# Loading two rows of an expert's w1 per partition with one DMA, in a hybrid RG-LRU, sparse-attention and MoE layer

## The chip, the cores and the metric

The kernel runs on one core of a Trainium2 chip. The metric is the device time of one execution in microseconds (us), and the median over several runs is what kernels are compared by. The engines are called as the profile calls them: PE (TensorE; PEld is its weight loads), DVE (VectorE), ACT (ScalarE), POOL (GpSimd) and SP (SyncE, which here only issues DMAs). Sixteen DMA engines move data between the memory of the chip (HBM) and the core's SBUF.

## The reference

One layer works on 512 tokens of 1024 features, in f32. After a modulated RMSNorm come two parallel branches (an RG-LRU recurrence and an attention over the best 128 keys of each query), whose joined output is added to x. Then follows a mixture of 32 experts, of which each token uses 4. This is the part that the change touches:

```python
def moe_ffn(h, w_router, b_router, w1, b1, w2, b2):
    logits = (h @ w_router + b_router).astype(jnp.float32)
    top_val, top_e = lax.top_k(logits, TOPK_EXPERTS)          # 4 of 32
    gates = jax.nn.softmax(top_val, axis=-1).astype(h.dtype)
    ...
    def expert_block(args):
        tok, gate, e = args
        u = h_pad[tok] @ w1[e] + b1[e]                        # (1024) -> 2048
        u_glu = jnp.minimum(u[:, ::2], SWIGLU_LIMIT)
        u_lin = jnp.clip(u[:, 1::2], -SWIGLU_LIMIT, SWIGLU_LIMIT)
        act = u_glu * jax.nn.sigmoid(SWIGLU_ALPHA * u_glu) * (u_lin + 1)
        return (act @ w2[e] + b2[e]) * gate[:, None]          # (1024) -> 1024
```

Each expert has 8 MB of w1 and 4 MB of w2, so the 32 experts read 384 MB of weights, each byte once.

## The kernel before

The first 450 us or so do the norm, the input projection, the two branches, the output projection and the router. The rest of the time goes to the experts.

**The experts in order.** The experts are ranked by how many tokens chose them (the first two by number, so that their weights can be loaded before the router is done), and each gets 1 to 4 blocks of 32 token rows, by a fixed list. The list `NBS` of blocks in the order of work is 3, 3, 4, 2, 3, 2, 3, 4, 2, 3, 2, 3, and so on, and ends with 2, 1, 2, 1. There are 86 blocks in all. A loop at the end of the program takes tokens that found no room; it ran zero times in the profiled execution.

**One expert.** The loop from L974 interleaves neighbours. For expert j it gathers token rows two experts ahead (L859, POOL), loads w1 of j and multiplies (`up`, L888), applies the gated activation (`glu`, L893 to L897, DVE and ACT), turns the tokens of the next expert (`turn_x`, L867) and makes its bias (L874), loads w2 of expert j - 1 and multiplies (`down`, L915 and L921), scales and adds the result to the output by an accumulating indirect DMA (`add_out`, L930 and L932), and turns its own activations (`turn_act`, L905). Weights are the moving operand: `up` goes through 8 rows k of w1, each 128 x 2048, and for each row and block issues four matmuls of 32 columns by 512. The trace holds two records for each such f32 matmul, so a row of w1 with 4 blocks is 32 records, and with 1 block 8.

**The weight slots.** Weights lie in a ring of nine SBUF slots of 16 KB per partition:

```python
slots_at = (164, 148, R[0], R[1], R[3], R[2], R[5], R[4], R[6])
...
t = [mem(kb + 8 * j, blocks, n) for j in range(2)]
for j in range(2):
    nc.sync.dma_start(t[j], src(j))
```

Each slot holds two tiles of 8 KB per partition, and each tile is the target of one DMA of 1 MB: one row k of w1 (128 partitions x 8 KB) or one quarter of w2 (also 8 KB per partition). In HBM, partition p's eight rows of w1 lie one behind the other, 64 KB in a piece (`w1_of`, L950), and the DMA of one row takes 8 KB out of it. An expert takes six slots, four for w1 and two for w2.

**What sets the order.** All weight DMAs stand in one queue, SP's, in the order that the framework's scheduler gives them. Such a DMA is issued when three things hold: the DMA before it on SP has been issued; PE is through with what lay in that tile (the wait on PE); and the DMA that last used the same completion semaphore has landed. There are eight of these semaphores (DMAHW0 to DMAHW7), taken in turn, so at most eight of SP's DMAs are under way. PE waits for each weight DMA at the first matmul that reads its tile. The order of the instructions on every engine is also the scheduler's.

Of the kernel before, what the change touches and what calls it, by code (L numbers as in the profile page):

```python
# [18 lines left out]
S, D, H, HD, E, FF = 512, 1024, 8, 64, 32, 1024  # L19
# [18 lines left out]
def layer(ctx, tc, x, c, w_ada, b_ada, norm1_g, w_in, conv_w, conv_b, w_rg_a, b_rg_a, w_rg_x, b_rg_x,  # L38
          lru_lambda, q_norm_g, k_norm_g, kidx_norm_g, rg_out_g, attn_out_g, w_out, norm2_g,
          w_router, b_router, w1, b1, w2, b2, out, dbg=None):  # L40
    nc = tc.nc
    V, A, T, G = nc.vector, nc.scalar, nc.tensor, nc.gpsimd
# [15 lines left out]
    bk = [psp.tile([128, 512], F32, name=f"bank{i}") for i in range(8)]  # L58
# [6 lines left out]
    def mem(kb, *shape, dt=F32):  # L65

        n = 1
        for d in shape:
            n *= d
        key = (kb, n, dt)  # L70
        if key not in views:
            assert kb * 1024 % 32 == 0 and kb * 1024 + n * (2 if dt == BF else 4) <= nc.sbuf_usable_end - base
            views[key] = nc.alloc_sbuf_tensor_at(f"mem{len(views)}", [128, n], dt, offset=base + int(kb * 1024)).ap()
        v = views[key]
        if len(shape) > 1:
            names = "abcd"[:len(shape)]
            v = v.rearrange(f"p ({' '.join(names)}) -> p {' '.join(names)}", **dict(zip(names, shape)))
        return v
# [133 lines left out]
    xT = [mem(112 + 2 * k, S) for k in range(4)] + [mem(131.375 + 2 * k, S) for k in range(4)]  # L212
# [16 lines left out]
    for v in range(2):  # L229
        for k, g in [(k, g) for k in range(KD) for g in (2 * v, 2 * v + 1)]:  # L230
            t = ada[2 * (g // 2) + k // 4][:, k % 4, 512 * (g % 2):512 * (g % 2) + 512]
# [472 lines left out]
    BT = 32  # L704
# [15 lines left out]
    nslot = [0]  # L720
    slots_at = (164, 148, R[0], R[1], R[3], R[2], R[5], R[4], R[6])
# [97 lines left out]
    def wslot(blocks, n, src):  # L819
        nslot[0] += 1  # L820
        kb = slots_at[(nslot[0] - 1) % len(slots_at)]
# [3 lines that stand above are left out]
        return t  # L825
# [49 lines left out]
        A.copy(biasb[j % 2], p)  # L875

    def load_up(src):
        return [t for q in range(4) for t in wslot(1, 2 * FF, lambda j: src[:, 2 * q + j:2 * q + j + 1, :])]

    def load_down(src):  # L880
        return [t for q in range(2) for t in wslot(2, D, lambda j: src[:, 2 * q + j])]
# [1 line left out]
    def up(j, w, nb):  # L883
        xT = xTs[j % 2]
        for k in range(KD):
            for b in range(nb):
                for n in range(4):
                    T.matmul(bk[b][32 * n:32 * n + 32, :], xT[:, k, BT * b:BT * b + BT], w[k][:, 0, n * 512:(n + 1) * 512],  # L888
                             start=(k == 0), stop=(k == KD - 1))

    def glu(j, nb):
# [62 lines left out]
    def expert(j):  # L954

        if j < 2:
            return slice(j, j + 1)
        if j not in whose:
            whose[j] = nc.values_load(ids[0:1, j:j + 1], engines=[mybir.EngineType.SP], min_val=0, max_val=E - 1)
        return bass.ds(whose[j], 1)  # L960
# [13 lines left out]
    for j in range(E + 1):  # L974
        nb = NBS[j] if j < E else 0
        if j + 2 < E:
            gather(j + 2, xg_of(j + 2), NBS[j + 2])
        if j < E:
            w = load_up(w1_of(expert(j)))
            up(j, w, nb)  # L980
            glu(j, nb)
        if j + 1 < E:
            turn_x(j + 1, xg_of(j + 1), NBS[j + 1])
            bias(j + 1, bias_col(j + 1))
        if j == 0:
            gated_bias()
        if j:
            down(load_down(w2_of(expert(j - 1))), NBS[j - 1])
            add_out(j - 1, NBS[j - 1])
        if j < E:  # L990
            turn_act(nb)
        if j % 4 == 0 and j + 4 < E:
            route(j + 4, 4)
# [20 lines left out]
    with tc.For_i(0, blocks, 1):  # L1014
# [39 lines left out]
        turn_x(0, 0, 4)  # L1054
        bias(0, selb1)
        up(0, load_up(w1_of(bass.ds(ev, 1))), 4)
        glu(0, 4)
        turn_act(4)
# [26 lines left out]
```

## Time and profile before

| what | value |
|---|---|
| median of 3 runs | 1475.12 us (1473.19 to 1480.09) |
| profiled execution | 1474.65 us, of which the span from first to last instruction is 1472.7 us |
| PE busy | 1372.4 us (93% of the span), 10907 matmul records |
| of these `up`, L888 | 622.9 us, 5504 records |
| of these `down`, L915 and L921 | 270.6 and 60.7 us, 2304 and 448 records |
| DVE, ACT, POOL busy | 34%, 18%, 15% of the span |
| loads of w1 and w2 | 384 DMAs of 1024 KB, issued by SP at L824 |
| hardware queue of SP (q1) | 75582 packets, 453.73 MB, 76.9% of the 16 engines' time |
| mean granted clock of PE | 0.958 |

The busy time of an engine is the union of its instructions, each record lasting until the modelled end of its matmul, so PE can be "busy" while a matmul shares the array with three others. The share of the DMA engines is the summed time of their packets over 16 engines, and can pass 1 a little, because a packet begins shortly before the one ahead of it is done. In the strips of the page a slice is 36.8 us, and a digit is tenths.

### The profile page before, as it was taken

The numbers are of one execution on the slowest core, as the hardware profiler recorded it, in microseconds if no ns is written. First come the engines' busy times: TensorE is split into PE (matmuls) and PEld (weight loads), VectorE is DVE, ScalarE is ACT, GpSimd is POOL, SyncE is SP. The second block draws the span as 40 slices with busy tenths as digits, with TensorE's granted clock in tenths as the row PEclk, the third lists the DMA queues.
The fourth block names the chain that finished last, engine by engine and source line by source line (L and its number), as shares of the span: only waits on it lengthen the run. The fifth ranks groups of instructions, "written<-read, shape, count | busy, mean of one in ns | idle before, by whom it ended". The sixth has DMA issues, their size and how long they took to land. (4 is left out here: it accounts for less than half of the span.)

```text
span 1472.7 us, 26489 instructions
## 1 busy us (share of the span) xinstructions
PE 1372.4 (93%) x10907; PEld 622.2 (42%) x10907; DVE 498.2 (34%) x1266; ACT 265.1 (18%) x538; POOL 228.1 (15%) x248
## 2 busy tenths in 40 slices
PE   5899999999779999999999999999999999999984
PEld 2755787777623343333433333333333333333220
DVE  2668986845624122212222122122132112212211
ACT  2544653532201010000010010001010010100100
POOL 3313621711100111011101011000101011110100
PEclk9999999958689999999999999999999999999996
DMA  9667213007578999999999999999999999999995
GB/s 361 213 212 261 93 58 115 22 29 292 208 281 353 379 384 409 372 403 408 404 398 403 417 403 399 401 405 398 413 389 404 405 411 407 399 389 390 413 404 199
DMA packets 87274, 482.40 MB, mean 328 GB/s; under 512 B 11974, under 2 KB 14214, under 8 KB 37902
## 3 DMA queue, kind: packets, MB, share of 16 engines
q1 hardware_dynamic: 75582, 453.73, 76.9%
q0 software_dynamic: 10560, 24.68, 6.9%
q10 hardware_dynamic: 1008, 2.25, 0.4%
q8 instruction: 88, 1.44, 0.4%
q14 instruction: 36, 0.29, 0.1%
HBM read 465.14 MB, written 15.48 MB: 326 GB/s over the span
## 5 line engine op out<-in xcount | busy, mean ns | idle before, releaser
L888 PE MATMUL bank<-mem,mem 128*32 128x512 f32 x5504 | 622.9, 595 | 2.8 <-DMA mem<-in_w_dram 2.8
L888 PEld LDWEIGHTS bank<-mem,mem 128*32 128x32 f32 x5504 | 174.7, 110 | 373.8 <-issue 359.1
L915 PE MATMUL bank<-mem,mem 128*32 128x512 f32 x2304 | 270.6, 597 | 0.0
L893 DVE TENSOR_TENSOR bank<-bank,mem 128x512 f32<-128x512 f32 x86 | 59.9, 697 | 450.4 <-PE bank L888 450.3
L932 POOL DMA_INDIRECT out_dram<-mem,idx_h x50 | 76.7, 1534 | 733.1 <-DVE mem L930 573.6
L915 PEld LDWEIGHTS bank<-mem,mem 128*32 128x32 f32 x2304 | 88.2, 110 | 144.5 <-issue 133.6
L895 ACT ACTIVATE mem<-bank 128x256 f32<-128x256 f32 x86 | 33.1, 385 | 559.1 <-DVE bank L893 559.1
L157 PE MATMUL bank<-mem,mem 128*128 128x512 f32 (+1 forms) x320 | 114.6, 359 | 4.1 <-DVE mem L537 3.1
L158 PE MATMUL bank<-mem,mem 128*128 128x512 f32 (+1 forms) x320 | 112.4, 351 | 0.0
L159 PE MATMUL bank<-mem,mem 128*128 128x512 f32 (+1 forms) x320 | 111.4, 348 | 0.0
L930 DVE SCALAR_TENSOR_TENSOR mem<-bank,gate_h,mem 128x512 f32<-128x512 f32 x36 | 27.0, 750 | 213.2 <-PE bank L915 204.5
L157 PEld LDWEIGHTS bank<-mem,mem 128*128 128x128 f32 x320 | 61.8, 194 | 17.6 <-issue 4.8
L158 PEld LDWEIGHTS bank<-mem,mem 128*128 128x128 f32 x320 | 61.9, 193 | 11.7 <-issue 5.0
L159 PEld LDWEIGHTS bank<-mem,mem 128*128 128x128 f32 x320 | 61.7, 193 | 11.5 <-issue 5.6
L859 POOL DMA_INDIRECT mem<-h_d,idx_all x32 | 30.5, 954 | 222.8 <-PE bank L867 151.3
L921 PE MATMUL bank<-mem,mem 128*32 128x512 f32 x448 | 60.7, 593 | 2.3 <-SPq L1014 1.3
L867 PEld LDWEIGHTS bank<-ident,mem 128*128 128x128 f32 (+2 forms) x256 | 33.2, 196 | 62.7 <-issue 28.5
L867 PE MATMUL bank<-ident,mem 128*128 128x128 f32 (+2 forms) x256 | 42.5, 294 | 17.9 <-DMA mem<-h_d,idx_all 9.3
L868 DVE COPY mem<-bank 128x512 f32<-128x512 f32 (+2 forms) x32 | 18.0, 563 | 115.1 <-PE bank L867 112.7
L906 ACT COPY mem<-bank 128x512 f32<-128x512 f32 (+1 forms) x32 | 18.3, 573 | 207.5 <-PE bank L915 108.9
L153 POOL TENSOR_TENSOR mem<-mem,mem 128x512 fp32r<-128x512 f32 x24 | 34.4, 1453 | 89.8 <-ACT mem L152 89.7
L905 PEld LDWEIGHTS bank<-ident,mem 128*128 128x128 f32 x172 | 24.3, 207 | 38.3 <-issue 22.9
(327 smaller groups left out, 1212.8 us busy)
## 6 DMA issues: line engine op xcount, KB each, us to landing
mem<-in_w_dram SPq DMA_DIRECT2D x384, 1024.0 KB
mem<-in_w_ada_dram SPq DMA_DIRECT2D x16, 1024.0 KB
mem<-in_w_in_dram SPq DMA_DIRECT2D x20, 512.0 KB
mem<-in_w_ada_dram SPq DMA_DIRECT2D x3, 2048.0 KB
mem<-in_x_dram SPq DMA_DIRECT2D x8, 512.0 KB
mem<-in_w_out_dram SPq DMA_DIRECT2D x8, 512.0 KB
mem<-in_w_ada_dram SPq DMA_DIRECT2D x4, 512.0 KB
mem<-in_w_in_dram SPq DMA_DIRECT2D x8, 256.0 KB
```

The lines of the kernel that those rows point to most:

```text
L153: (sub or V).tensor_sub(lo, src, hi)
L157: T.matmul(p, ah, bh, start=(k == 0), stop=False)
L158: T.matmul(p, al, bh, start=False, stop=False)
L159: T.matmul(p, ah, bl, start=False, stop=(k == n - 1))
L859: G.indirect_dma_start(out=xgs[to][a], out_offset=None, in_=h2_d, in_offset=bass.IndirectOffsetOnAxis(ap=idx_all[a, r:r + 1], axis=0))
L867: T.transpose(p[:, k, 0:n], xgs[frm][0:n, 4 * q + k::KD], ident[0:n, 0:n])
L888: T.matmul(bk[b][32 * n:32 * n + 32, :], xT[:, k, BT * b:BT * b + BT], w[k][:, 0, n * 512:(n + 1) * 512], start=(k == 0), stop=(k == KD - 1))
L893: V.tensor_add(bk[b], bk[b], biasb[j % 2])
L895: A.activation(act[:, b], u[:, :, 0], AF.Gelu_apprx_sigmoid)
L915: T.matmul(bk[6 + b // 2][o:o + 32, :], aT[:, b, c, BT * n:BT * n + BT], w[n][:, c, m * 512:(m + 1) * 512], start=(n + c == 0), stop=(n == ...
L921: T.matmul(bk[6 + nb // 2][o:o + 32, :], aT[:, nb - 1, c, BT * n:BT * n + BT], w[n][:, c, m * 512:(m + 1) * 512], start=(n == 0), stop=(n ...
L932: G.indirect_dma_start(out=out_half, out_offset=bass.IndirectOffsetOnAxis(ap=idx_h[a, h, j:j + 1], axis=0), in_=ys[h][a], in_offset=None, ...
```

## The change

`load_up` no longer goes through `wslot`. It takes a slot of the ring as before, but as one tile of 2 x 2048 per partition, and fills it with one DMA of rows 2q and 2q + 1 of w1. Since the two rows lie one behind the other in HBM and in the tile, the DMA moves one piece of 16 KB per partition. `up` takes the two halves of the tile as rows. The loads of w2 (`load_down`) keep their two tiles and two DMAs per slot. The ring, its nine slots and the order in which slots are taken are unchanged.

```diff
     def load_up(src):
-        return [t for q in range(4) for t in wslot(1, 2 * FF, lambda j: src[:, 2 * q + j:2 * q + j + 1, :])]
+
+        w = []
+        for q in range(4):
+            nslot[0] += 1
+            t = mem(slots_at[(nslot[0] - 1) % len(slots_at)], 2, 2 * FF)
+            nc.sync.dma_start(t, src[:, 2 * q:2 * q + 2, :])
+            w += [t[:, j] for j in range(2)]
+        return w
...
-                    T.matmul(bk[b][32 * n:32 * n + 32, :], xT[:, k, BT * b:BT * b + BT], w[k][:, 0, n * 512:(n + 1) * 512],
+                    T.matmul(bk[b][32 * n:32 * n + 32, :], xT[:, k, BT * b:BT * b + BT], w[k][:, n * 512:(n + 1) * 512],
                              start=(k == 0), stop=(k == KD - 1))
```

On SP, the loads of expert 3's w1 and expert 2's w2 stand like this before; the last number is the tile's size, the register rows between the DMAs are left out, and in the brackets DMAHW is a completion semaphore and PE the release of the tile:

```order
L959 TENSOR_LOAD ids
...
L824 DMA mem_78<-in_w_dram 128x2048 [waits DMAHW0_49,PE_49]
...
L824 DMA mem_79<-in_w_dram 128x2048 [waits DMAHW1_49,PE_49]
...
L824 DMA mem_3563<-in_w_dram 128x2048 [waits DMAHW2_49,PE_49]
...
L824 DMA mem_3564<-in_w_dram 128x2048 [waits DMAHW3_49,PE_49]
...
L824 DMA mem_3216<-in_w_dram 128x2048 [waits DMAHW4_49,PE_49]
...
L824 DMA mem_3217<-in_w_dram 128x2048 [waits DMAHW5_49,PE_49]
...
L824 DMA mem_3220<-in_w_dram 128x2048 [waits DMAHW6_49,PE_49]
...
L824 DMA mem_3221<-in_w_dram 128x2048 [waits DMAHW7_49,PE_49]
```

And the same place after the change, with the four loads of w2 that follow:

```order
L966 TENSOR_LOAD ids
...
L883 DMA mem_133<-in_w_dram 128x4096 [waits PE_49]
...
L883 DMA mem_103<-in_w_dram 128x4096 [waits DMAHW6_49,DMAHW5_49,PE_49]
...
L883 DMA mem_3216<-in_w_dram 128x4096 [waits PE_49]
...
L883 DMA mem_3218<-in_w_dram 128x4096 [waits DMAHW7_49,PE_49]
...
L824 DMA mem_3966<-in_w_dram 128x2048 [waits DMAHW0_49,PE_49]
...
L824 DMA mem_3967<-in_w_dram 128x2048 [waits DMAHW1_49]
...
L824 DMA mem_3970<-in_w_dram 128x2048 [waits DMAHW2_49,PE_49]
...
L824 DMA mem_3971<-in_w_dram 128x2048 [waits DMAHW3_49]
```

Eight loads with a release each became four, each with one release for both rows; and where a pair of w2 tiles follows a w1 tile in its slot, only the first of the pair waits for PE, since the whole tile is given back at once.

The other place is the end of the program on PE. These are the last matmuls of the last expert, which has one block (`up` in bank_65), and of the two `down` steps behind it (bank_71), before the change:

```order
L888 MATMUL bank_65<-mem_78,mem_2672 32x512 x4
L888 MATMUL bank_65<-mem_79,mem_2672 32x512 x4
L905 MATMUL bank_69<-ident,mem_2934 128x128
L915 MATMUL bank_71<-mem_3563,mem_2931 32x512 x8
L905 MATMUL bank_69<-ident,mem_2934 128x128
L915 MATMUL bank_71<-mem_3564,mem_2931 32x512 x8
...
L921 MATMUL bank_71<-mem_3220,mem_2931 32x512 x4
L921 MATMUL bank_71<-mem_3221,mem_2931 32x512 x4
L921 MATMUL bank_71<-mem_3224,mem_2931 32x512 x4
L921 MATMUL bank_71<-mem_3225,mem_2931 32x512 x4
```

And after it:

```order
L895 MATMUL bank_65<-mem_134,mem_2672 32x512 x8
L895 MATMUL bank_65<-mem_133,mem_2672 32x512 x8
L922 MATMUL bank_71<-mem_3548,mem_2931 32x512 x8
L912 MATMUL bank_69<-ident,mem_2934 128x128 x2
L922 MATMUL bank_71<-mem_3549,mem_2931 32x512 x8
...
L928 MATMUL bank_71<-mem_9397,mem_2931 32x512 x4
L928 MATMUL bank_71<-mem_9398,mem_2931 32x512 x4
L928 MATMUL bank_71<-mem_3966,mem_2931 32x512 x4
L928 MATMUL bank_71<-mem_3967,mem_2931 32x512 x4
```

The last two rows of w1 now come in one tile, and the scheduler has put the first quarter of the `down` step of the expert before between `up` and the transposes of the activations (L905, now L912), where the transposes came first.

## Rows read from the trace of the kernel before

**Rows 1.** The page: DMA busy digits, rates in 40 slices, SP's hardware queue.
```profile
DMA  9667213007578999999999999999999999999995
GB/s 361 213 212 261 93 58 115 22 29 292 208 281 353 379 384 409 372 403 408 404 398 403 417 403 399 401 405 398 413 389 404 405 411 407 399 389 390 413 404 199
...
q1 hardware_dynamic: 75582, 453.73, 76.9%
```

**Rows 2.** Engine busy time by stretch; last three columns: PE clock, DMA share, GB/s.
```profile
core 0: us, PE busy (x) PEld busy (x) DVE busy (x) ACT busy (x) POOL busy (x), PEclk, DMA share, GB/s
...
480.00:505.00 25.00, 25.00 (x233) 8.82 (x229) 2.42 (x4) 1.17 (x2) 3.09 (x2) 1.00 1.02 398
505.00:530.00 25.00, 25.00 (x232) 10.16 (x228) 8.44 (x17) 3.56 (x8) 2.54 (x2) 1.00 0.97 349
...
700.00:900.00 200.00, 197.14 (x1764) 69.41 (x1760) 42.62 (x115) 17.98 (x38) 21.26 (x16) 1.00 1.02 405
...
1325.00:1350.00 25.00, 25.00 (x236) 7.68 (x232) 5.43 (x12) 1.54 (x4) 0.00 (x0) 1.00 0.99 391
...
1400.00:1436.00 36.00, 31.38 (x285) 9.65 (x281) 5.28 (x10) 2.31 (x5) 2.98 (x2) 0.99 1.02 404
...
1450.00:1455.00 5.00, 3.12 (x28) 0.66 (x24) 0.75 (x1) 0.37 (x1) 1.56 (x1) 1.00 0.67 199
```

**Rows 3.** What PE waited for, 520 to 1472 us: total, times, longest (two rows).
```profile
PE bank L888 <- DMA mem<-in_w_dram: 2.8, 2, 2.1
...
PE bank L921 <- SPq L1014: 1.3, 1, 1.3
```

**Rows 4.** PE in order of time, the end: start, length, what, [idle before <-releaser].
```profile
1426.61 5.33 PE L888 MATMUL bank<-mem,mem 128*32 128x512 f32 x48
1432.70 1.07 PE L888 MATMUL bank<-mem,mem 128*32 128x512 f32 x8 [0.76 <-DMA mem<-in_w_dram]
1435.85 1.93 PE L888 MATMUL bank<-mem,mem 128*32 128x512 f32 x8 [2.08 <-DMA mem<-in_w_dram]
...
1440.48 3.64 PE L915 MATMUL bank<-mem,mem 128*32 128x512 f32 x16
...
1451.14 2.94 PE L921 MATMUL bank<-mem,mem 128*32 128x512 f32 x24 [0.96 <-ACT mem L906]
...
1455.42 1.07 PE L921 MATMUL bank<-mem,mem 128*32 128x512 f32 x8 [1.34 <-SPq L1014]
```

**Rows 5.** DMA packets and mean rate, 37 to 43 us (w_in, 2 KB pieces).
```profile
DMA packets 1268, 2.44 MB, mean 407 GB/s; under 512 B 77, under 2 KB 77, under 8 KB 1268
```

**Rows 6.** The same, 16 to 26 us (w_ada, 4 KB pieces).
```profile
DMA packets 1067, 4.21 MB, mean 421 GB/s; under 512 B 40, under 2 KB 40, under 8 KB 1066
```

**Rows 7.** The same, 826 to 849 us (expert weights alone, 8 KB pieces).
```profile
DMA packets 1345, 9.79 MB, mean 426 GB/s; under 512 B 152, under 2 KB 152, under 8 KB 152
```

**Rows 8.** What SP waited for, 480 to 530 us (all its rows).
```profile
SPq L824 <- PE bank L888: 27.1, 10, 3.9
SPq L824 <- PE bank L921: 15.6, 7, 3.5
```

**Rows 9.** PE in order of time: `up` of an expert with 4 blocks.
```profile
485.72 27.67 PE L888 MATMUL bank<-mem,mem 128*32 128x512 f32 x256
```

**Rows 10.** What SP waited for, 640 to 1320 us (the two longest).
```profile
SPq L824 <- PE bank L888: 242.8, 123, 5.5
SPq L824 <- DMA mem<-in_w_dram: 143.9, 85, 4.1
```

**Rows 11.** One line's instructions on SP: count, ns min/median/max, first and last start.
```profile
L824 SPq DMA_DIRECT2D mem<-in_w_dram x384: 327/333/643, 301.0 to 1435.9; - x192
```

**Rows 12.** DMA issues of POOL: count and median us from issue to landing.
```profile
out_dram<-mem,idx_h POOLq DMA_INDIRECT x50, 9.1
...
mem<-h_d,idx_all POOLq DMA_INDIRECT x32, 8.6
```

**Rows 13.** What POOL waited for, 520 to 1472 us (the two longest).
```profile
POOL out_dram L932 <- DVE mem L930: 563.6, 30, 37.6
POOL out_dram L932 <- DMA out_dram<-mem,idx_h: 119.5, 14, 10.0
```

## The prediction

> **What bounds the kernel now.** I began with the strips of the page [rows 1]. From the fourteenth slice (478 us) on the DMA engines stand at 9 in every slice but the last, at 353 to 417 GB/s; before that they are often half idle. SP's hardware queue carries 453.73 MB, of which the expert weights are 402.7 MB (384 loads of 1 MB). So the last two thirds are a stage that reads weights. The busy times by stretch [rows 2] say that it is full: the DMA share is 1.02 in nearly every stretch, and only 0.97 in 505 to 530 us and 0.99 in 1325 to 1350. PE is busy nearly all the time too (197.14 of 200 us), so I asked which of the two is late. In 520 to 1472 us PE waits for a weight DMA in two places, 2.8 us in all [rows 3], and both are at the end: 0.76 and 2.08 us at the last two rows of the last `up` [rows 4]. The last eight matmul records begin at 1455.42, after 1.34 us of waiting that is put down to SP; the share of 0.67 in 1450 to 1455 [rows 2] shows that weights were still landing, so this is the last load of w2. So PE and the DMA engines run level for most of the stage: PE works from a store of loaded weights, uses it up over the last experts, which have 1 or 2 blocks, and the end is set by the landing of the last load. An edit of the loads counts by how it moves that landing. It gains or loses there nearly one to one, until PE's own chain takes over.
>
> **The change part by part.**
>
> *Longer pieces.* The trace has no piece above 8 KB, so I read what each doubling gave in stretches where one kind of load runs alone: 2 KB pieces 407 GB/s [rows 5], 4 KB 421 [rows 6], 8 KB 426 [rows 7]. Per load of 1 MB (1.0486 MB of the counter) that is 2.576, 2.491 and 2.461 us, steps of 0.085 and 0.030 us. A fixed cost per piece would halve with each doubling, so I take half of the last step, 0.015 us per MB. It counts for the loads of w1 inside the full stage: the first two experts' lie in the half-idle slices before it [rows 1], and 30 experts x 8 MB = 240 MB remain. Gain: 240 x 0.015 = 3.6 us. Ends: nothing at all, or as much again as the step before, 240 x 0.030 = 7.2 us. On the other side, pieces of 16 KB could run at the rate of 4 KB ones, a loss of 7.2 us; the rows, which only rise, speak against that, and I keep it as a rival.
>
> [...]
>
> *Coarser release.* A load of w1 can now start only when PE is through with both rows that lay in the slot, and a w2 pair behind a w1 tile too. This costs only where the DMA engines have caught up with PE's releases. That is the stretch from 480 to 530 us: there SP waits 17 times, 42.7 us in all, each time for PE and never for a DMA [rows 8], and the share falls to 0.97 [rows 2]. `up` of the first expert with 4 blocks takes 27.67 us for 8 rows [rows 9], 3.46 us per row, and a load takes 2.46, so the queue runs dry. A starved stream is done one load after the last release: 2.46 us before, and two loads, 4.92 us, after the change. So it leaves this stretch 2.5 us later, and since the share is full from there on, the delay stays until the end. Ends: 0 (if the order of the early loads happens to cover it) and one row of PE, 3.5 us. Elsewhere the release is covered: between 640 and 1320 us 85 of SP's waits are for a DMA [rows 10], namely the load eight before, and while seven or eight loads of 2.46 us are queued, one release that comes 1.7 to 3.5 us later changes nothing. The near miss is 1325 to 1350 us (0.99); a stream starved there would again be late by one load against PE, which is not added to the first delay but replaces it.
>
> *Coarser landing.* PE's first row of a pair waits for both. In the body weights lie ready long before (no wait in rows 3 but the two at the end). At the end it counts: row 6 of the last `up` now waits until 1435.85 with row 7, so `up` ends 1.07 us later [rows 4]. Behind it stands a `down` quarter of 16 records before the transposes, which covers the activation; then the `down` steps follow, the last 24 records before the final wait ending at 1454.08 + 1.07 = 1455.15. The last load lands at 1455.4, so this is hidden, with 0.3 us to spare. If the last load came over 0.3 us earlier than everything before it, PE would be the late one; but all loads of the end shift together.
>
> *SP and the semaphores.* 128 fewer issues of 333 ns each [rows 11] take 42.6 us off SP, which mostly waits: nothing. Eight loads under way now hold up to 12 MB instead of 8, since four of each twelve-MB expert are double; the 143.9 us of waiting for the load eight before will shrink and turn into waiting for PE. It also gains nothing, since the engines are full during those waits.
>
> *POOL's DMAs.* Gathers and scatters take turns with the weights on the same engines, and a piece of 16 KB takes about twice the 0.308 us of one of 8 KB (8192 B at a sixteenth of 426 GB/s). A scatter of 128 rows is 8 pieces per engine, so it may land 8 x 0.3 = 2.4 us later than the 9.1 us now [rows 12]. POOL has cover: it waits 563.6 us for results and only 119.5 for an earlier scatter [rows 13], and gathers run two experts ahead. Cost: 0; without that cover 2.4 us per scatter on POOL.
>
> *Sum.* -3.6 + 2.5 = -1.1 us. The profiled execution took 1474.65 us and would take 1473.5. The median of the runs, 1475.12, is 0.5 us above it, so I predict 1474.0. A difference under 0.5% (7.4 us) can't be told from none in this kernel; this is well within.
>
> **The rivals.**
>
> *The pieces are cut, or the cut doesn't matter (1477.6).* If the hardware moves 16 KB as two pieces of 8 KB, or a piece's cost is nil, the change doesn't do what it says, and only the coarser release is left: 1475.1 + 2.5. For it: nothing in the trace is longer than 8 KB. Against it: so far the piece followed the contiguous run, whatever its length. [...]
>
> *Longer pieces help most where queues share the engines (about 1463).* Alone the weights run at 426 GB/s, but over whole stretches it is 404 or 405 [rows 2, 7], because gathers and scatters take turns with them. The gap, 5% of some 980 us, is 50 us. If engines turn once per piece, half as many w1 pieces could save a part; a quarter of the gap is 12 us, 1475.1 - 12 = 1463. For it: the gap is real. Against it: POOL's pieces are as many as before, and each still costs its time. Beyond some 8 us PE's own chain at the end would limit it, because only the waits of rows 4 can close.
>
> *16 KB pieces run slower (about 1485).* An engine that can't hold a piece of 16 KB between its read and its write would stall inside it. Place: every load of w1 in the full stage; price: back to the rate of 4 KB pieces, 7.2 us, and the release's 2.5 us on top, 1475.1 + 9.7 = 1484.8. It decides as soon as the rate of w1 alone falls below 421 GB/s. For it: no row shows such a piece. Against it: the three steps of rows 5 to 7.
>
> **How the numbers follow.** I give the forecast 0.62 (its own range 1470 to 1478), the cut pieces 0.13, the gain in shared stretches 0.13, the slower pieces 0.12. The first two are within 0.5%, so no change has 0.75; faster has 0.13 and slower 0.12. For 8 in 10 the range takes the first two and reaches part of the way to the others: from 1466 (the full 7.2 us and a little of the waits at the end) to 1482 (no gain, the release at its dear end of 3.5 us, the landing's 1.1 us, and a small part of the slower pieces).
>
> **What would show it.** Pieces: the hardware queue's packets fall by 32768 / 2 = 16384 if pieces of 16 KB are really moved; a stretch of w1 alone at 428 to 429 GB/s confirms the 0.015 us, 426 or less refutes it. Release: the share between 505 and 530 us falls below 0.97, and the full stretch begins later. Landing: two waits at the end merge into one of 3 to 4 us before the last pair of rows. SP: its waits for weight DMAs nearly vanish before 1400 us. I am wrong if rates in the shared stretches move by over 1%, up or down, or if PE begins to wait for weights before 1400 us.

## The result, and the profile after

The changed kernel takes 1487.12 us (median of 6 runs, 1483.16 to 1489.11) against 1475.48 (6 runs, 1471.37 to 1480.09) for the kernel before on the same chip: ratio 1.0083, 95% interval 1.0057 to 1.0108. It is slower by 0.8%, where 1474.0 us and no change were forecast. The profiled execution has a span of 1486.1 us.

The strips and SP's queue on the page of after, against [rows 1]:

```profile
PEclk9999999959689999999999999999999999999997
DMA  9667213008569999999999999999999999999994
GB/s 361 207 220 263 78 57 114 22 1 329 218 236 366 387 400 408 387 405 404 406 393 401 419 389 398 398 390 388 411 376 401 390 402 396 392 389 393 412 407 169
...
q1 hardware_dynamic: 57150, 453.72, 76.1%
```

The queue moves the same bytes in 18432 fewer packets. Of these, 16384 are pieces of w1, so pieces of 16 KB are really moved whole; the other 2048 are packets of 4 B, 16 for each of the 128 DMAs that are gone, and e3 below, with 2 MB loads of 8 KB pieces, lacks just these (73534 packets). The strips look alike. A loss of 12 us in 1486 does not show in tenths; it has to be looked for by stretch. The busy times by stretch in after, columns as in [rows 2]:

```profile
505.00:530.00 25.00, 25.00 (x236) 10.12 (x232) 8.45 (x17) 3.56 (x8) 2.54 (x2) 1.00 0.95 368
700.00:900.00 200.00, 195.65 (x1732) 68.14 (x1726) 42.95 (x116) 17.94 (x38) 21.09 (x16) 0.99 1.02 402
900.00:1100.00 200.00, 192.08 (x1688) 63.91 (x1684) 42.85 (x116) 17.57 (x37) 22.12 (x17) 0.97 1.01 395
1100.00:1300.00 200.00, 193.72 (x1734) 64.72 (x1730) 38.72 (x87) 17.67 (x37) 19.56 (x15) 0.99 1.01 394
```

and the last two of these stretches in before:

```profile
900.00:1100.00 200.00, 193.05 (x1734) 65.66 (x1730) 43.44 (x117) 18.09 (x38) 20.57 (x16) 1.00 1.02 400
1100.00:1300.00 200.00, 193.97 (x1740) 64.50 (x1732) 38.80 (x87) 17.11 (x36) 20.99 (x16) 1.00 1.02 402
```

Two things differ. The rate falls by 5 and 8 GB/s (1.3 and 2.0%, over the 1% that the prediction set as a sign of being wrong), while the DMA share only goes from 1.02 to 1.01. And PE's granted clock, 1.00 in all three long stretches of before, falls to 0.99, 0.97 and 0.99: there are short times at half the clock (1.2 instead of 2.4 GHz). What PE waited for in 520 to 1486 us in after, against [rows 3]:

```profile
PE bank L895 <- DMA mem<-in_w_dram: 5.6, 2, 3.1
PE bank L928 <- SPq L1021: 4.8, 3, 2.4
```

PE still waits for weights at the end only, but there for 10.4 us instead of 4.1. SP's longest waits in 640 to 1320 us are now for PE alone (the same view as [rows 10]; no row of it names a DMA):

```profile
SPq L883 <- PE bank L895: 202.8, 39, 14.0
SPq L824 <- PE bank L895: 171.3, 40, 6.3
```

So in the body PE doesn't wait for weights, and the weights wait for PE's releases. A lower rate is then more likely to follow from PE than to hold it up, and PE's own lateness has to be explained. It is made in two places. The first lies before the stage that the prediction looked at. Three rows of after in order of time (ScalarE, GpSimd and TensorE, with what ended their idle time):

```profile
372.38 1.06 ACT L652 ACTIVATE mem<-mem 128x1024 f32<-128x1024 f32 x1 [4.94 <-DMA h_d<-mem]
...
405.28 1.01 POOL L859 DMA_INDIRECT mem<-h_d,idx_all  x1 [8.22 <-DMA h_d<-mem]
...
415.19 1.97 PE L867 MATMUL bank<-ident,mem 128*128 128x128 f32 x8 [12.09 <-DMA mem<-h_d,idx_all]
```

These are the router's stores of normalised rows (`h_d`, 512 KB per tile) and the first gather of such rows. Each of these rows waits for one of them, and all but the third store, which lands in 2.9 us, share the DMA engines with the first experts' w1. The second place is PE's order from about expert 9 on (experts are counted from 0 here), which the scheduler changed together with the loads: 1022 of the 6512 matmuls stand elsewhere. The experiments take the two places apart.

### The profile page after: what moved, and what is told of

Same layout as the page of the kernel before. It is cut to its first block, busy times and chain, and to the rows that moved or that the text cites. A ratio compares the mean times of both kernels' runs of the same rounds, so it can differ in the third digit from the quotient of the medians.

```text
span 1486.1 us, 25951 instructions
## 1 busy us (share of the span) xinstructions
PE 1375.2 (93%) x10907; PEld 620.7 (42%) x10907; DVE 497.3 (33%) x1266; ACT 265.0 (18%) x538; POOL 228.0 (15%) x248
## 5 line engine op out<-in xcount | busy, mean ns | idle before, releaser
L895 PE MATMUL bank<-mem,mem 128*32 128x512 f32 x5504 | 622.6, 600 | 5.6 <-DMA mem<-in_w_dram 5.6
L895 PEld LDWEIGHTS bank<-mem,mem 128*32 128x32 f32 x5504 | 176.7, 111 | 392.1 <-issue 372.8
L158 PEld LDWEIGHTS bank<-mem,mem 128*128 128x128 f32 x320 | 61.7, 193 | 11.6 <-issue 5.0
L867 PE MATMUL bank<-ident,mem 128*128 128x128 f32 (+2 forms) x256 | 43.1, 300 | 21.5 <-DMA mem<-h_d,idx_all 12.1
L867 PEld LDWEIGHTS bank<-ident,mem 128*128 128x128 f32 (+2 forms) x256 | 33.3, 197 | 54.5 <-issue 20.1
L868 ACT COPY mem<-bank 128x512 f32<-128x512 f32 (+2 forms) x32 | 15.5, 485 | 140.0 <-PE bank L867 98.0
```

The costliest lines, as they stand in the source:

```text
L158: T.matmul(p, al, bh, start=False, stop=False)
L867: T.transpose(p[:, k, 0:n], xgs[frm][0:n, 4 * q + k::KD], ident[0:n, 0:n])
L868: (V.tensor_copy if q else A.copy)(xTs[j % 2][:, 4 * q:4 * q + 4, 0:n], p[:, :, 0:n])
```

## The experiments

Theory A: the new order of PE's work, with the drops of the clock that come with it, costs the time. Theory B: the 16 KB pieces cost it. Theory C: the 2 MB that are loaded and released together cost it. To hold an order, each engine's instructions were chained in the sequence that the other kernel has. This is a list of numbers in the kernel, and no semaphore comes with it. With that, order, DMA size and piece length can be varied one at a time:

| order of the engines | 1 MB, 8 KB pieces | 2 MB, 8 KB pieces | 2 MB, 16 KB pieces |
|---|---|---|---|
| of before | before: 1474.4 | e3: 1473.3, ratio 1.0005 [0.9986, 1.0025] | e1: 1479.5, ratio 1.0038 [1.0021, 1.0056] |
| of after | e2: 1478.1, ratio 1.0022 [1.0002, 1.0041] | e4: 1482.8, ratio 1.0068 [1.0044, 1.0092] | after: 1487.1, ratio 1.0083 [1.0057, 1.0108] |

Medians in us; each ratio is to runs of the kernel before on the same chip as that kernel (for after another set, median 1475.48).

**e1: the order undone.** The changed kernel, held to the order of before:

```diff
+    for eng, count, runs in RUNS:
+        mine = [i for i in nc.cur_bb.bb.instructions if str(i.engine).split('.')[-1] == eng and i.opcode not in skip]
+        want = [mine[f + n] for f, m in runs for n in range(m)]
+        for a, b in zip(want, want[1:]):
+            tc.add_manual_dep(b, a.name, ...)
```

> The changed kernel, but the instructions of TensorE, VectorE, ScalarE and GpSimd held in the order that they have in the kernel before (1022 of TensorE's 6512 matmuls stand elsewhere in the changed kernel). Theory A (the new order of TensorE's work, with the clock drops that come with it, lost the 11 us): back to the kernel before, ratio 0.997 to 1.002, about 1475 us, full clock from 452 to 1435 us. Theory B (16 KB pieces move fewer bytes where other queues share the engines) and theory C (a slot that is freed and filled only by whole 2 MB): still about 1485 to 1488, ratio 1.006 to 1.009.

Measured: 1479.48 us, ratio 1.0038 [1.0021, 1.0056], between what the theories said. By the ratios a little over half of the loss goes with the order; the rest stays.

**e2: the order alone.** The kernel before, held to the order of after (same edit, other list).

> The kernel before with its 1 MB DMAs of 8 KB pieces, but with the order that the four engines have in the changed kernel. Theory A: 1485 to 1489 us, ratio 1.006 to 1.010, with the drops of the clock at 755, 984, 1093 and 1264 us. Theories B and C: 1474 to 1477, ratio 0.998 to 1.002.

Measured: 1478.08 us, ratio 1.0022 [1.0002, 1.0041]: again between. The drops of the clock that theory A named are there, each at the same place in PE's work, but by the medians the whole order costs some 4 us with 1 MB loads, not 12.

**e3: 2 MB loads of 8 KB pieces, old order.** Rows 0 and 2, 1 and 3, and so on, share a slot, so the pieces don't join:

```diff
-            nc.sync.dma_start(t, src[:, 2 * q:2 * q + 2, :])
+            nc.sync.dma_start(t, src[:, q + q // 2 * 2:q + q // 2 * 2 + 3:2, :])
```

(`up` takes the rows of xT in the same sequence.)

> 2 MB per DMA and one release for it, but of rows that don't adjoin in memory (0 with 2, 1 with 3, and so on), so pieces of 8 KB; all four engines in the order of the kernel before. Theory A: about 1475 us, ratio 0.997 to 1.002, and not apart from the run with 16 KB pieces in that order. Theory B: 1475 to 1478. Theory C: 1485 to 1488, ratio 1.006 to 1.009.

Measured: 1473.29 us, ratio 1.0005 [0.9986, 1.0025]. Theory C falls for the old order: loading and releasing 2 MB at once costs nothing there that is clear of noise. Against e1 only the length of the pieces differs: 6.2 us by the medians, 5.2 by the two spans (1471.2 and 1476.4).

**e4: the same in the new order.**

> The same 2 MB DMAs of two 8 KB pieces that don't adjoin, in the order that the four engines have in the changed kernel. Theory A: 1485 to 1489 us, ratio 1.006 to 1.010, like the changed kernel. Theory B: 1475 to 1478, ratio 0.999 to 1.002. Theory C: 1485 to 1488.

Measured: 1482.78 us, ratio 1.0068 [1.0044, 1.0092]. By the medians the order costs 9.5 us with 2 MB loads and 3.7 with 1 MB loads, as if the coarse release cost more where PE is late. The traces don't bear that out. The first records of `up` for three experts (counted from 0) start at these times in us, the last row is the span:

| | before | e3 | e1 | e2 | e4 | after |
|---|---|---|---|---|---|---|
| order | old | old | old | new | new | new |
| expert 2 | 485.72 | 480.80 | 485.32 | 478.97 | 481.25 | 487.29 |
| expert 9 | 717.31 | 712.39 | 716.91 | 710.55 | 712.84 | 718.88 |
| expert 17 | 979.03 | 974.12 | 978.63 | 979.35 | 981.62 | 987.62 |
| end | 1472.7 | 1471.2 | 1476.4 | 1476.3 | 1479.5 | 1486.1 |

Two of these starts as the traces show them, expert 9's in before and expert 17's in after (expert 2's in before is the line of [rows 9]):

```profile
717.31 1.05 PE L888 MATMUL bank<-mem,mem 128*32 128x512 f32 x2
```

```profile
987.62 12.71 PE L895 MATMUL bank<-mem,mem 128*32 128x512 f32 x100
```

From expert 2 to 9 all six take 231.59 us, and from 9 to 17 the old order takes 261.7 and the new one 268.7 to 268.8, whatever the size of the loads and pieces. So PE sets the pace there, and the order alone costs 7.0 us. From expert 2 to the end the old order takes 987.0 to 991.1 us in the nine traced runs that have it throughout, the new one 997.3 (e2), 998.3 (e4) and 998.8 (after). In these single executions the order costs 10.3 us with 1 MB loads and 7.9 and 7.7 with 2 MB loads, and long pieces cost 0.7 or less. That the coarse release adds to the order's cost is therefore not shown. Why the medians of before and e2 lie only 3.7 us apart stays open; before reached expert 2 6.8 us later than e2, in the same order up to there. No run holds the kernel before to its own order, so what the chains themselves do to the time wasn't measured either.

*Where the long pieces cost.* The same three rows as above, in e3 (8 KB pieces):

```profile
368.02 1.06 ACT L652 ACTIVATE mem<-mem 128x1024 f32<-128x1024 f32 x1 [2.78 <-DMA h_d<-mem]
...
398.54 1.00 POOL L859 DMA_INDIRECT mem<-h_d,idx_all  x1 [6.50 <-PE bank L952]
...
407.71 1.97 PE L867 MATMUL bank<-ident,mem 128*128 128x128 f32 x8 [9.64 <-DMA mem<-h_d,idx_all]
```

and in e1 (16 KB pieces, nothing else different):

```profile
369.98 1.06 ACT L652 ACTIVATE mem<-mem 128x1024 f32<-128x1024 f32 x1 [4.62 <-DMA h_d<-mem]
...
402.67 1.01 POOL L859 DMA_INDIRECT mem<-h_d,idx_all  x1 [8.00 <-DMA h_d<-mem]
...
413.29 1.97 PE L867 MATMUL bank<-ident,mem 128*128 128x128 f32 x8 [12.59 <-DMA mem<-h_d,idx_all]
```

e1 is 1.96 us late at the first row (the store before it lands later), 4.13 at the second (the last store too), 5.58 at the third (the gather too), and 5.2 at the end of the program. In e3 the second row names PE, but in both runs the gather starts some 0.95 us after the last store has landed (e3: issued at 386.98, landed 10.6 us later; e1: 389.61 and 12.1), so it waits for the store in e3 too. The stores' landing, 345 to 415 us, in e3, e1 and e8 (pieces of 8, 16 and 2 KB of w1 beside them; the last column is the median from issue to landing in us):

```profile
h_d<-mem POOLq DMA_DIRECT2D x4, 512.0 KB, 8.6
```

```profile
h_d<-mem POOLq DMA_DIRECT2D x4, 512.0 KB, 10.8
```

```profile
h_d<-mem POOLq DMA_DIRECT2D x4, 512.0 KB, 6.8
```

A store of 128 rows is 8 small pieces per engine. A 16 KB piece takes about 0.303 us longer than one of 8 KB (16384 B at a sixteenth of 430 GB/s against 8192 B at a sixteenth of 427, both rates below). If each small piece waits for one piece of w1, that is 8 x 0.303 = 2.4 us more with 16 KB and, by the same sum, 1.8 less with 2 KB; measured are 2.2 and 1.8. The median of four mixes stores with and without weights beside them; the first store alone, which has weights beside it in every run, lands after 8.3 to 9.2 us in the eight runs with 8 KB pieces there, with 1 MB loads as with 2 MB ones, 10.6 to 10.9 in the three with 16 KB and 7.0 to 7.1 in the three with 2 KB. The Trainium skill, page "DMA: Bandwidth & Descriptors", section "Queues, rings and completion order", says that an engine takes turns between queues by packets of typically 9 to 17 descriptors. As an estimate from that, a store that waits once, for such a packet of 9, would be 2.7 us later, so these rows agree with it about as well and don't tell the two apart.

Four runs test this place.

**e5: 16 KB pieces from the third expert on.** Old order, 2 MB loads; only the first two experts' pieces are kept apart, so that they are of 8 KB:

```diff
-            w = load_up(w1_of(expert(j)))
-            up(j, w, nb)
+            w = load_up(w1_of(expert(j)), j < 2)
+            up(j, w, nb, j < 2)
```

> Old order on the four engines, 2 MB per DMA; pieces of 8 KB (rows that don't adjoin) for the first two experts, of 16 KB from the third on. Theory B1 (16 KB pieces cost only where the router's stores and the first gathers, on which TensorE waits, share the engines with them, at 345 to 415 us; from L640's start to the first turn of gathered rows 68.8 us with 16 KB pieces, 62.3 to 64.2 with 8 KB): like the run with 8 KB pieces throughout in that order, 1472 to 1475 us, and that stretch 62 to 64 us. Theory B2 (16 KB pieces cost bytes in the long stretch where all queues share): 1477 to 1480.

Measured: 1474.76 us, ratio 1.0014 [0.9999, 1.0029]. B1 holds: the long pieces of the 30 later experts cost nothing that is clear of noise, and gain nothing either. The pieces of the two experts before them make the difference to e1. The stretch is short again: PE's first turn at 406.81 us, from VectorE's first instruction at L640 at 347.61 it is 59.2 us, against 65.8 in e1, 60.3 in e3, 61.1 in before and 65.6 in after (the expectations count from the queue's semaphore 3.1 us ahead of that instruction).

**e6 and e7: loads held.** The second expert's last three slots of w1 wait until the first two gathers have landed; in e6 with 16 KB pieces and 2 MB loads, in e7 with the DMAs of before:

```diff
+            if 6 <= nslot[0] <= 8:
+                tc.add_manual_dep(d.ins, held.ins.name, mybir.DependencyInfo(mybir.DependencyClass.Sync, ...))
```

> Old order, 2 MB per DMA, 16 KB pieces throughout, but the second expert's last three w1 loads wait until the first two gathers have landed (about 10 us later than now), so that the router's last store and these gathers share the engines with no weights. Theory B1: the last store falls from 11.5 to 2 to 5 us, the first gather from 9.6 to 3 to 5, the first turn of gathered rows comes 8 to 12 us earlier, and the whole kernel with it: 1467 to 1473 us against 1479.5 without the wait. Rival (these transfers aren't what is late): no earlier, 1478 to 1481. Rival (the held loads come too late): TensorE waits for weights at the second expert, 1480 or more.

> The kernel before (1 MB DMAs, 8 KB pieces, its order), with the same wait for the second expert's last w1 loads. Theory B1: the stretch to the first turn of gathered rows falls from 62 to 64 to some 54 to 57 us, and the kernel to 1464 to 1469 us, ratio 0.993 to 0.997, the fastest so far. Rivals: 1473 to 1476 (not what is late), or over 1476 (weights late).

Measured: e6 1469.77 us, ratio 0.9973 [0.9960, 0.9986], 9.7 us under e1; e7 1464.56 us, ratio 0.9949 [0.9928, 0.9969]. Both times lie where B1 said; the stretch became even shorter (51.1 us in e7, where 54 to 57 were expected). GpSimd and PE in e7, which answer to the last two of the rows above:

```profile
394.22 1.01 POOL L862 DMA_INDIRECT mem<-h_d,idx_all  x1 [2.12 <-PE bank L811]
...
398.44 1.97 PE L870 MATMUL bank<-ident,mem 128*128 128x128 f32 x8 [0.30 <-DMA mem<-h_d,idx_all]
```

The gather starts 7.2 us after the last store is issued instead of 11.6 in e3 (its row names PE; in e6, where the store's landing can be read, it still starts 0.95 us after that), and PE waits for the gather for 0.30 us instead of 9 to 12. The stretch is 10.0 us shorter than in before, and the medians of e7 and before differ by 8.7 us. Nothing of it is given back in the body.

**e8: 2 KB pieces for the first two experts.** The kernel before, its order; each of their w1 loads is cut into four by columns:

```diff
+            if n == 2 * FF and nslot[0] <= 8:
+                for m in range(4):
+                    nc.sync.dma_start(t[j][:, :, m * 512:(m + 1) * 512], src(j)[:, :, m * 512:(m + 1) * 512])
+                continue
```

> The kernel before, its order, but the first two experts' w1 in DMAs of 256 KB with 2 KB pieces. If the cost goes by the length of the piece in front (16 KB 68.8 us, 8 KB 62.3 to 64.2 in that stretch), a quarter of 8 KB takes off 3 to 5 us more: 58 to 61 us there, 1470 to 1472 us in all. Rival (from 8 KB down nothing more is gained, or so many small DMAs come late): 1474 to 1478.

Measured: 1463.66 us, ratio 0.9939 [0.9924, 0.9954], the stretch 51.0 us. Direction right, size missed: 9.6 us came off, not 1 to 3. The rows say where, against before: the last store is issued 35.1 us into the stretch (40.7 before), the gather 7.9 us after that (11.3), and PE's first turn 8.0 us after the gather (9.1). My sum had only scaled the step from 16 to 8 KB. The 5.6 us before the last store have two parts. From the second store's issue to the third's, e8 takes 9.38 us and before 11.62: ScalarE's wait ahead of L652 is 0.97 us instead of 3.26, and in both it goes on 0.4 to 0.5 us after the first store's landing. From the third store's issue to the fourth's, e8 takes 8.52 us and before 11.92, with few weights in flight in either; PE's granted clock is what differs, here in before and in e8 (columns as in [rows 2]):

```profile
380.19:392.11 11.92, 8.53 (x40) 8.42 (x41) 6.23 (x39) 4.37 (x12) 2.30 (x3) 0.50 0.11 44
```

```profile
374.65:383.17 8.52, 6.10 (x52) 5.73 (x52) 6.67 (x39) 4.48 (x12) 2.29 (x2) 1.00 0.17 68
```

The same part takes 10.13 us at a clock of 0.69 in e12 and 11.56 at 0.60 in e11, both with 2 KB pieces too. So these 3.4 us of the traced execution go with the clock and aren't owed to the piece length alone. The loads of e8 are also smaller, with at most 2 MB under way instead of 8, which no run parts from the length of the pieces.

Now PE's order. The matmuls ahead of expert 20's `up` in order of time, in e3 (old order):

```profile
1081.23 0.71 PE L867 MATMUL bank<-ident,mem 128*128 128x128 f32 x4 [0.76 <-ACT mem L913]
1081.87 1.92 PE L895 MATMUL bank<-mem,mem 128*32 128x512 f32 x16
1083.61 0.40 PE L874 MATMUL bank<-b1t,permb 96*32 96x512 bf16 x4
1084.69 0.34 PE L839 MATMUL bank<-pay,mem 128*128 128x5 bf16 x8 [0.68 <-ACT mem L875]
1084.96 1.92 PE L895 MATMUL bank<-mem,mem 128*32 128x512 f32 x16
1086.82 0.36 PE L839 MATMUL bank<-pay,mem 128*128 128x5 bf16 x8
```

and in e4 (order of after, same DMAs):

```profile
1087.45 0.40 PE L874 MATMUL bank<-b1t,permb 96*32 96x512 bf16 x4 [0.67 <-ACT mem L868]
1088.53 0.34 PE L839 MATMUL bank<-pay,mem 128*128 128x5 bf16 x8 [0.68 <-ACT mem L875]
1089.05 1.32 PE L839 MATMUL bank<-pay,mem 128*128 128x5 bf16 x8 [0.17 <-DVE mem L837]
1090.72 0.69 PE L867 MATMUL bank<-ident,mem 128*128 128x128 f32 x2 [0.34 <-DVE rtv L844]
1091.34 5.75 PE L895 MATMUL bank<-mem,mem 128*32 128x512 f32 x32
```

In the old order rows of `up` (L895) stand between the turns (L867), the bias (L874) and the routing of later experts (L839), and cover their waits. In the new order the small matmuls stand in a row, each with its wait, and `up` begins at 1091.34 instead of 1081.87, 9.5 us later, of which 5.0 were there at expert 19. Its first 32 records then take 5.75 us where 16 take 1.92 in e3: the clock is at half from 1088.8 to 1095.6 us. What this does to the weights, by stretch, columns as in [rows 2], in e3, in e2 (new order, 1 MB loads) and in e4 (new order, 2 MB loads):

```profile
985.00:1030.00 45.00, 44.32 (x408) 16.60 (x404) 9.14 (x18) 5.00 (x11) 4.96 (x4) 1.00 1.00 397
1436.00:1470.00 34.00, 13.52 (x98) 3.19 (x98) 2.18 (x3) 0.96 (x2) 2.98 (x2) 0.76 0.51 196
```

```profile
985.00:1030.00 45.00, 44.78 (x416) 13.97 (x412) 8.82 (x17) 3.87 (x8) 2.20 (x2) 1.00 1.00 383
1436.00:1470.00 34.00, 17.25 (x106) 3.26 (x106) 3.72 (x6) 1.34 (x3) 2.99 (x2) 0.67 0.58 222
```

```profile
985.00:1030.00 45.00, 45.00 (x412) 13.14 (x404) 8.13 (x16) 2.70 (x6) 1.59 (x1) 0.98 0.98 369
1436.00:1470.00 34.00, 17.07 (x118) 3.61 (x114) 3.73 (x6) 1.34 (x3) 2.99 (x2) 0.77 0.73 282
```

Behind the late PE the rate falls to 383 with 1 MB loads and to 369 GB/s with 2 MB loads, where the share falls below 1 as well; SP waits for PE alone here in all three runs. That some DMA engines run dry before the next 2 MB are released is likely, but not shown. The bytes are missing at the end: 282 - 196 = 86 GB/s over 34 us are 2.9 MB more in e4's last stretch, which at 405 GB/s is, as an estimate, 7.2 us of its 8.3 us of longer span. PE waits for weights there for 9.4 us in e4, 7.9 in e2 and 4.8 in e3.

**e9: the new order, but the old one from expert 15 to 20.** e4 with that part of the list taken from before.

> 2 MB DMAs of 8 KB pieces in the changed kernel's order, but with the old order in one stretch, from the fifteenth to the twentieth expert (414 of TensorE's 6512 matmuls, 36 of VectorE's instructions, 5 of ScalarE's), where TensorE fell from 1.8 to 9.3 us behind the same DMAs in the old order (1482.8 us against 1473.3). Theory A1 (TensorE's lateness there lets the weight queue run low, and that isn't made good): TensorE 1 to 3 us behind at the twentieth expert, the half-clock stretches at 980 and 1089 us gone or shorter, 1474 to 1478 us. Rival (what the new order costs lies elsewhere, or is made good later anyway): 1481 to 1484 us.

Measured: 1477.24 us, ratio 1.0031 [1.0017, 1.0045]. A1 holds: 5.5 of e4's extra 9.5 us go with this one stretch, where the rate is back at 392 GB/s (985 to 1030 us) and PE is 1.2 us behind e3 at expert 20. Between e9 and e3 some 4 us by the medians are left. The traced execution of e9, the fastest of its twelve, doesn't show them (989.9 us from expert 2 to the end, 990.4 in e3), so where they arise is open.

**e10: the new order, its waits filled.** e4 with 15 more matmuls in the waits of two such rows of small matmuls, ahead of experts 17 and 20 (the numbers in the expectation count from 0, as this text does):

```diff
+        for _ in range({17: 5, 20: 10}.get(j, 0)):
+            d = T.matmul(bk[3][0:32, :], ident[:, 0:32], g2h, start=True, stop=True)
```

> 2 MB DMAs of 8 KB pieces in the changed kernel's order throughout, with 15 more matmuls (32 columns by 512, into a bank that nothing uses then) put where TensorE waits among its small matmuls ahead of the seventeenth and the twentieth expert; nothing else is moved. If the clock falls there because TensorE stands idle: the half-clock stretches of 6.8 us at 980 and 1089 us go, TensorE is 3 us earlier after each, 1476 to 1480 us. If it falls because the small matmuls themselves ask little: the stretches stay, 1482 to 1485 us.

Measured: 1486.90 us, ratio 1.0104 [1.0088, 1.0121]: slower than e4, which neither side said. The stretch at expert 17 in e4, without the fillers:

```profile
979.60:986.40 6.80, 6.80 (x36) 2.61 (x40) 1.23 (x7) 0.94 (x2) 1.90 (x2) 0.50 1.05 379
```

and in e10, with them, together with the first three of them in order of time:

```profile
982.00:989.00 7.00, 7.00 (x67) 2.27 (x70) 0.47 (x2) 0.23 (x1) 1.00 (x2) 1.00 1.04 334
```

```profile
974.12 2.74 PE L895 MATMUL bank<-mem,ident 128*32 128x512 f32 x6
```

The first half of the expectation holds: both half-clock stretches are gone, so PE's waits among its small matmuls are what they followed. (The fillers are long matmuls themselves, so waiting and thin work aren't fully parted; and the stretch at 1260 us, which is not filled, is 6.8 us long instead of 3.4.) The price of a filler was wrong: three of them took 2.74 us, 0.91 each, and I had taken 0.22 from rows of `up` (24 in 5.33 us, [rows 4]), where four matmuls run side by side. The ten fillers ahead of expert 20 made its `up` begin at 1095.44, another 4.1 us later than in e4, and the kernel became 4.1 us slower. So lateness of PE in this place is paid nearly in full at the end.

A half-clock stretch costs PE half its length. e4 and e2 have the same order, but between experts 9 and 11 only e2 has one, 3.4 us long; from the start of expert 9's `up` to that of expert 11's e2 takes 66.0 us and e4 64.3, 1.7 less. The Trainium skill, page "TensorE: Matmul & The Clock Gate", section "Terms", gives the same sum (time at the lower level times the missing share), and the rows agree. In the body after has four of them, 20.4 us together, so 10.2 us of PE's time; before has none, e1 one and e3 two of 3.4 us.

**e11 and e12: both costs taken off.** e11 is e8 (2 KB pieces, here for the first five slots) with e7's hold. e12 is the change itself with these two and the old order: 16 KB pieces and 2 MB loads for everything else.

> The kernel before, its order, the first expert's w1 and the first quarter of the second's in DMAs of 256 KB with 2 KB pieces, and the rest of the second's held until the first two gathers have landed. By the rows of the two runs that did one of these: the first two stores 6.3 us as with 2 KB pieces, the last store and the gathers 3 to 5 us as with the held loads, so some 2 to 3 us less than the held loads alone: 1461 to 1463 us, ratio 0.991 to 0.994. Rival (the two take away the same wait): 1464 to 1466 us.

> The change with its two costs taken off: 2 KB pieces for the first five slots of w1, the next three held until the first two gathers have landed, 16 KB pieces by 2 MB DMAs for all the rest, the four engines in the old order. If TensorE sets the pace once both costs are gone (the pieces' higher rate, 430 against 427 GB/s alone, is worth nothing): like the run with 1 MB DMAs and 8 KB pieces, 1461 to 1464 us. If the rate counts (the 3.6 us of the prediction): 1457 to 1460. If long pieces or 2 MB releases still cost something in the body: 1465 to 1469.

Measured: e11 1462.73 us, ratio 0.9931 [0.9907, 0.9954]; e12 1462.35 us, ratio 0.9944 [0.9927, 0.9960]. Both beat the kernel before, and they don't differ clearly from each other, from e8 (0.9939) or from e7 (0.9949); that the two measures add up is not shown. Whether the body's w1 comes in pieces of 8 or 16 KB makes no difference to the time that is clear of noise, although the long ones are faster by themselves. 821 to 835 us, w1 nearly alone, in e3 and in e1:

```profile
DMA packets 778, 5.97 MB, mean 427 GB/s; under 512 B 50, under 2 KB 50, under 8 KB 50
```

```profile
DMA packets 415, 6.01 MB, mean 430 GB/s; under 512 B 47, under 2 KB 47, under 8 KB 47
```

## Why the prediction was wrong

- **What bounds the kernel: half right, and the wrong half decided.** The last load does land last, and at the end PE waits for weights. But what moves that landing is PE: in the body PE sets the pace (231.59 us from expert 2 to expert 9 in all 14 traced runs), the loads wait for its releases, and the faster w1 of e5 brought nothing. A DMA share of 1.02 was read as a limit. It is the summed time of packets and doesn't say who waits for whom; it only went to 1.01 in after while the rate fell by 8 GB/s [rows 2]. (A slip in the reading of [rows 1]: from the fourteenth slice on the lowest rate is 372 GB/s; 353 is the thirteenth slice. Nothing hangs on it.)
- **Longer pieces, -3.6 us: the rate was right, its worth was not.** The forecast was 428 to 429 GB/s, measured is 430. Since PE sets the pace, e5 gains nothing from it over e3, nor e12 over e11. The step also left out the first two experts' pieces because they lie in half-idle slices. That is where they did harm.
- **POOL's DMAs, 0 us: the first step that failed.** The size was right: 2.4 us later per 8 pieces, measured 2.2. The cover was looked up for gathers and scatters in 520 to 1472 us [rows 13] and taken to hold for the whole program. At 345 to 415 us there is none: ScalarE waits for a store, the gather for the last store, PE for the gather, each later by 1.4 to 2.2 us, in all 5.6. This is worth 4 to 6 us by the medians (by the ratios to before, 0.33% in the old order, clear of noise, and 0.15% in the new one, which isn't), and theory B as I first put it (a cost in the shared stretches of the body) is refuted by e5.
- **The order of PE's work: no step at all, the second failure.** The scheduler's new order was read only on SP and at the program's end. By the medians it costs 3.7 us with 1 MB loads and 9.5 with 2 MB loads, by the traces 10.3 and 7.9 from expert 2 on.
- **Coarser release, +2.5 us at 480 to 530 us: wrong place.** The share there falls to 0.95 as said, against 0.97 [rows 2], but e3 has the coarse release and is not later than before. Whether it costs where PE is already late is open: e4 against e2 is 4.7 us by the medians and 1.0 by the traces from expert 2 on.
- **SP's issues and the semaphores: right.** SP's waits for DMAs have vanished from the body [rows 10], and nothing came of it. The coarser landing can't be judged in after, where PE and the loads reach the end in another state (PE waits twice at the last `up`, 2.44 and 3.12 us, where one wait was forecast); e3 has it too and is not later than before. The packets fell by the 16384 forecast pieces and by 2048 packets of 4 B that the forecast had left out.
- **The rivals.** The one on the slower side came within 2.3 us of the time, but by luck and not by its mechanism: the pieces were not slower, the rate of w1 alone rose. The cut pieces are refuted by the packets, the gain in shared stretches by e5.

By the two profiled spans the change costs 13.4 us, and since before reached the router 1.8 us later (351.39 against 349.59 us), 15.2 from there on: 4.5 in the router's stretch (65.6 against 61.1) and 10.7 behind it, which by the traces is nearly all the order: 7.0 of it arise between expert 9 and expert 17.

## What to carry to other kernels

When a bulk load's pieces grow, look for every small transfer that something waits for while that load is under way, in all stages and not only in the one that the load bounds: here their landing grew by about the piece's extra length times the number of small pieces. A change of DMA sizes can make a scheduler rewrite the order of an engine that the change never names, so the orders of all engines are compared first, and small matmuls that lost their cover cost twice here, by the wait and by the clock. Whether the DMA engines or the compute engine set the pace is read from who waits for whom, not from a share near 1.

## What was not expected of the hardware

- The cheapest gain in this kernel had nothing to do with the body: 2 KB pieces for two experts (e8) take off 9.6 us, 3.4 of them with PE's clock in the traced execution, although 2 KB pieces are the slowest by rate (407 GB/s, [rows 5]).
- A matmul of 32 columns alone took 0.91 us, while four of them, into different strips of the array, took 1.07 us together in `up` [rows 4].
- A half-clock stretch is not tied to the order alone: in one and the same order before has none in the body, e1 one and e3 two, and the stretches cost PE 1.7 us each.
